# Moving the split weight tiles by multiples of 32 bytes in an fp32r decoder trunk on one core

## The chip, the core and the metric

The kernel runs on one NeuronCore of one Trainium2 chip, as one launch. The metric is the device time of one execution in microseconds (us). The whole of the core's work is done in one program: the sync engine (SP) issues nearly all loads, the tensor engine (PE) multiplies, the scalar engine (ACT), the vector engine (DVE) and GpSimd (POOL) prepare operands and take results out of PSUM.

## What is computed

The reference is a two-layer decoder trunk on 256 tokens of width 2048, in fp32. Layer 0 mixes by a gated spatial projection beside a 4-head attention into 256 memory tokens, layer 1 by 12-head latent attention beside the same kind of memory attention; after each comes an output projection and a gated feed-forward with a short causal convolution. Cut to the places where the weights enter:

```python
for l in range(DEPTH):                        # DEPTH = 2, N_A = 1
    if l == N_A:
        kv = rmsnorm(x, g_kv) @ w_kv_a
        ...
    h = rmsnorm(x, g_mix[l])
    ...
        z = h @ w_in_a[l]                     # 2048 x 3584 in layer 0, w_in_b 2048 x 1024 in layer 1
    ...
    mo = memory_attention(q_m, mem, g_mem[l], w_mem_kv[l])
    x = x + jnp.concatenate([main, mo], axis=-1) @ w_out[l]                    # 2048 x 2048
    x = x + conv_ffn(rmsnorm(x, g_ffn[l]), w_ffn_up[l], ..., w_ffn_down[l])    # 2048 x 11264, 5632 x 2048
return rmsnorm(x, g_final)
```

Nearly all arithmetic is in these projections: every weight is used once for 256 tokens.

## The kernel before, in words

**Split operands.** The data type fp32r runs through the PE in one pass but keeps fewer bits than fp32. The kernel therefore writes each fp32 operand as a sum of two fp32r numbers, high and low, and adds three products: high by high, high by low, low by high. Activations are split once per layer and stay in SBUF as one tile per use (`xhl`, `h`, `mainhl`, `memhl`, `qhl`, `chl`): per block of 128 features 512 columns, 256 tokens high and then 256 tokens low.

**Weights.** A weight is loaded, split and used in chunks of 128 partitions by at most 1024 columns (4096 bytes a partition). `chunk` (L92) does it: SP loads a `raw` tile (L101), ACT copies it into `whi` (L111, or L116 with a gain), which rounds it to fp32r, and DVE subtracts and writes the rest into `wlo` (L112, or L117). The three tags `raw`, `whi` and `wlo` have four buffers each in the pool `wp`, used in turn. Tiles of one tag lie one behind the other, and a tile may start at any multiple of 32 bytes of a partition. In the built program all twelve buffers begin 96 bytes past a multiple of 512, and so does every activation tile that the fp32r products read. The `whi` buffers are at 63072, 67168, 71264 and 75360, the `wlo` buffers at 79456 and on, each 4096 further.

**Products.** A projection is a slice of a weight matrix of 512 columns (or fewer), one call of `gemm_fm` (L171) or `gemm_tm` (L212); there are 99 such calls, of 96 or 128 matmuls each in the large ones. In `gemm_fm` the weights are the stationary operand (128 by 128) and the activations stream: `mm_fm` (L147) issues for each block a wide matmul of 512 columns, `whi` by high and low activations at once (L152), and a narrow one of 256 columns, `wlo` by the high activations into the second half of the same PSUM bank (L156). It issues all wide ones of two chunks, then all narrow ones, and turns the order for the next two chunks, so that 32 wide and 32 narrow matmuls alternate. In `gemm_tm` the activations are stationary and the weights stream, three matmuls of 512 columns for each block (L207, L208, L209); the memory values, the gate half of `w_in_a`, `w_uv` and the feed-forward's second matrix in layer 1 go this way. The queries of layer 1 call `chunk` directly, and one small block of `w_kv_a` goes through `stacked` (L123), which puts both parts into one tile.

**Order.** A scheduler sets the order on each engine from the program's data dependencies; it does not look at addresses. Dependencies are kept by semaphores: a `whi` buffer is written again when the last wide matmul that reads it is done, a `wlo` buffer after its last narrow one, and `raw` is loaded again when both halves of the split have read it.

**Scratch.** The program reserves 16384 bytes of each partition at address 0 as scratch of dynamic DMAs, ahead of all tiles.

The functions that the change touches, with the lines of the profile:

Of the kernel before, what the change touches and what calls it, by code (L numbers as in the profile page):

```python
# [9 lines left out]
F32R = mybir.dt.float32r  # L10
# [6 lines left out]
P = 128  # L17
# [52 lines left out]
class Kernel:  # L70
    def __init__(self, ctx, tc, t, out):
        self.tc, self.nc, self.t, self.out = tc, tc.nc, t, out
        self.ctx = ctx
        self.n = 0
        pool = lambda name, bufs=1, **k: ctx.enter_context(tc.tile_pool(name=name, bufs=bufs, **k))
        self.cp = pool("cp")
        self.wp = pool("wp")
        self.ap = pool("ap")
        self.ps = pool("ps", 8, space=bass.MemoryType.PSUM)
# [12 lines left out]
    def chunk(self, src, nk, ncol, gains=None, heads=None, raw=None):  # L92
        nc, n = self.nc, nk * ncol
        loaded = raw is not None
        if not loaded:
            raw = self.wp.tile([P, 1024], F32, tag="raw", name=self.uid("raw"), bufs=4)
        hi = self.wp.tile([P, 1024], F32R, tag="whi", name=self.uid("whi"), bufs=4)
        lo = self.wp.tile([P, 1024], F32R, tag="wlo", name=self.uid("wlo"), bufs=4)
        view = lambda x: x[:, :n].rearrange("p (k c) -> p k c", k=nk)
        if not loaded:  # L100
            nc.sync.dma_start(out=view(raw), in_=src)  # L101
        if heads is not None:

            s = view(raw).rearrange("p k (h c) -> p k h c", h=2)
            for c0, c1 in ((0, heads), (heads, ncol // 2)):
                o = lambda x: view(x)[:, :, 2 * c0 : 2 * c1].rearrange("p k (h c) -> p k h c", h=2)
                nc.scalar.activation(o(hi), s[:, :, :, c0:c1], AF.Copy)
                nc.vector.tensor_tensor(o(lo), s[:, :, :, c0:c1], o(hi).bitcast(F32), ALU.subtract)
            return view(hi), view(lo)
        if gains is None:  # L110
            nc.scalar.activation(hi[:, :n], raw[:, :n], AF.Copy)  # L111
            nc.vector.tensor_tensor(lo[:, :n], raw[:, :n], hi[:, :n].bitcast(F32), ALU.subtract)  # L112
        else:
            for k in range(nk):
                s = slice(k * ncol, (k + 1) * ncol)
                nc.scalar.activation(hi[:, s], raw[:, s], AF.Copy, scale=gains[k])  # L116
                nc.vector.scalar_tensor_tensor(  # L117
                    lo[:, s], raw[:, s], gains[k], hi[:, s].bitcast(F32), ALU.mult, ALU.subtract
                )
        return view(hi), view(lo)  # L120


    def stacked(self, src, nk, ncol, gains):  # L123
        nc, n = self.nc, nk * ncol
        raw, full = (self.wp.tile([P, 1024], F32, tag="raw", name=self.uid("raw"), bufs=4) for _ in range(2))
        nc.sync.dma_start(out=raw[:, :n].rearrange("p (k c) -> p k c", k=nk), in_=src)
        v3 = lambda x: x[:, :n].rearrange("p (k c) -> p k c", k=nk)
        g3 = gains.rearrange("p (k a) -> p k a", a=1).to_broadcast([P, nk, ncol])
        nc.vector.tensor_tensor(v3(full), v3(raw), g3, ALU.mult)
        blocks = []  # L130
        for i, tag in enumerate(("whi", "wlo")):
            w = self.wp.tile([P, 1024], F32R, tag=tag, name=self.uid(tag), bufs=4)
            half = slice(i * nk // 2, (i + 1) * nk // 2)
            w4 = w.rearrange("p (k o c) -> p k o c", o=2, c=ncol)
            nc.scalar.activation(w4[:, :, 0, :], v3(full)[:, half, :], AF.Copy)
            nc.vector.tensor_tensor(w4[:, :, 1, :], v3(full)[:, half, :], w4[:, :, 0, :].bitcast(F32), ALU.subtract)
            blocks += [w[:, j * P : (j + 1) * P] for j in range(nk // 2)]
        return blocks
# [29 lines left out]
            low(jobs)  # L168


    def gemm_fm(self, src, kbs, nblk, rhs, evict, nk=2, gain=None, hooks={}, raw=None):  # L171
        accs = [self.psum() for _ in range(nblk)]
        together = 1 if raw is not None else 2
        chunks = list(range(0, len(kbs), nk))
        groups = [chunks[i : i + together] for i in range(0, len(chunks), together)]

        def split(group):
            jobs = []
            for c in group:
                g = None if gain is None else [gain(kbs[c + i]) for i in range(nk)]  # L180
                hi, lo = self.chunk(src(kbs[c], nk), nk, nblk * P, g, raw=raw if c == 0 else None)
                for b in range(nblk):
                    cols = slice(b * P, (b + 1) * P)
                    for i in range(nk):
                        kk = c + i
                        jobs.append((accs[b], hi[:, i, cols], lo[:, i, cols], rhs(kbs[kk]), kk == 0, kk == len(kbs) - 1))
            return jobs

        ready = []
        for n, group in enumerate(groups):  # L190
            ahead = groups[n : n + 2] if raw is not None else [group]
            for g in ahead[len(ready) :]:
                ready.append(split(g))
                for f in hooks.get(-1, ()) if g is groups[0] else ():
                    f()
            self.mm_fm(ready.pop(0), n % 2 if raw is None else 0)
            for c in group:
                for f in hooks.get(c // nk, ()):
                    f()
        for b in range(nblk):  # L200
            evict(b, accs[b])
# [9 lines left out]

    def gemm_tm(self, src, nkb, ncol, lhs, evict, nk=2, gain=None, hooks={}, late=0):  # L212
        accs = [self.psum() for _ in range(2)]
        nch = nkb // nk
        order = lambda *engines: self.tc.manual_schedule(engines=set(engines)) if late else nullcontext()
        ET = mybir.EngineType

        def half(c, tb, hi, lo):
            for i in range(nk):
                k = c * nk + i  # L220
                self.mm_tm(accs[tb][:, :ncol], lhs(k), tb, hi[:, i, :], lo[:, i, :], k == 0, k == nkb - 1)

        kept = []
        with order(ET.PE):
            for c in range(nch):
                g = None if gain is None else [gain(c * nk + i) for i in range(nk)]
                hi, lo = self.chunk(src(c * nk, nk), nk, ncol, g)
                half(c, 0, hi, lo)
                if c < nch - late:
                    half(c, 1, hi, lo)  # L230
                else:
                    kept.append((c, hi, lo))
                for f in hooks.get(c, ()):
                    f()
            with order(ET.DVE, ET.Activation):
                if late:
                    evict(0, accs[0])
                for c, hi, lo in kept:
                    half(c, 1, hi, lo)
                if not late:  # L240
                    evict(0, accs[0])
                evict(1, accs[1])
# [113 lines left out]
    def gain(self, name, k, n=1):  # L356
        c = self.g[name] + k
        return self.gT[:, c : c + n]
# [741 lines left out]
```

## Time and profile before

| what | value |
|---|---|
| median of the 2 runs shown | 2103.38 us (2102.95 to 2103.81) |
| the profiled execution's own time | 2103.8 us |
| its span, first to last instruction | 2102.1 us |
| granted TensorE clock over the span | 0.999 |
| PE busy | 2090.7 us, 99% |
| DVE, ACT, POOL busy | 1460.8, 1140.1, 395.6 us |
| DMA: loaded from HBM | 387.88 MB |

The span leaves 1.7 us of the profiled execution outside the program's instructions. A matmul's record is longer than the time to the next one, since matmuls are pipelined: a run of n equal matmuls that the timeline gives as one piece lasts n-1 steps and one whole record. What a matmul costs the PE is the step. The span falls into stages: the start, the memory keys and values and layer 0's mixer up to some 355 us, the first feed-forward up to 1080 us, layer 1's mixer up to 1360 us, the second feed-forward to the end.

### The profile page before, as it was taken

Reading aid. Unit: us, or ns where it says so; the run is one execution under the profiler, and the core shown is the slowest. Engines: PE = TensorE matmul, PEld = TensorE weight load, DVE = VectorE, ACT = ScalarE, POOL = GpSimd, SP = SyncE. Lnnn points to the kernel's source line nnn. Section 1 sums busy time; section 2 is a strip of 40 time slices with the busy share of each in tenths; the row PEclk is TensorE's granted clock in tenths of the full one; section 3 lists DMA queues with packets and bytes.
Section 4 is the critical chain, followed back from the end, with each engine's and each line's share of the span. In section 5 each row is a group of like instructions: output and inputs, shape, how many; then the busy total and the mean of one; then the engine's idle time right before and its main releaser. Section 6 shows DMA issues by size and latency. Waiting matters only on the chain.

```text
span 2102.1 us, 30987 instructions
## 1 busy us (share of the span) xinstructions
PE 2090.7 (99%) x11608; PEld 1830.2 (87%) x11608; DVE 1460.8 (69%) x2147; ACT 1140.1 (54%) x1743; POOL 395.6 (19%) x387
## 2 busy tenths in 40 slices
PE   9999999999999999999999999999999999999998
PEld 8888888888888888888888888888888888888886
DVE  6755767777756777567788875777775677746775
ACT  6754654556535655445555664456553565535554
POOL 0100133312101211012244121421210122101220
PEclk9999999999999999999999999999999999999999
DMA  8565555555555565555555534555655556565554
GB/s 275 194 219 158 159 195 186 188 191 191 188 193 188 182 199 189 191 186 188 188 191 181 176 106 158 184 189 180 191 193 196 183 188 192 195 195 190 181 190 151
DMA packets 208092, 392.01 MB, mean 186 GB/s; under 512 B 14334, under 2 KB 23876, under 8 KB 207812
## 3 DMA queue, kind: packets, MB, share of 16 engines
q1 hardware_dynamic: 207364, 388.98, 56.9%
q8 instruction: 91, 1.49, 0.3%
q10 hardware_dynamic: 576, 1.05, 0.1%
q14 instruction: 61, 0.50, 0.1%
HBM read 387.88 MB, written 2.10 MB: 186 GB/s over the span
## 4 chain that ended last, share of the span: by engine, by line
PE 99%; DMA 0%; DVE 0%; ACT 0%; SPq 0%; issue 0%; DVEq 0%; ACTq 0%
PE ps L152 51%; PE ps L156 27%; PE ps L207 6%; PE ps L209 6%; PE ps L208 6%; PE ps L934 0%; PE ps L932 0%; PE ps L560 0%; PE ps L595 0%; PE ps L417 0%; DMA mtok<-in_mem 0%; PE ps L964 0%; PE ps L745 0%; PE ps L857 0%; PE ps L584 0%; PE ps L1036 0%
## 5 line engine op out<-in xcount | busy, mean ns | idle before, releaser
L112 DVE TENSOR_TENSOR wlo<-raw,whi 128x1024 fp32r<-128x1024 f32 x660 | 844.3, 1289 | 476.3 <-ACT whi L111 350.7
L111 ACT ACTIVATE whi<-raw 128x1024 fp32r<-128x1024 f32 x660 | 697.1, 1058 | 702.7 <-PE ps L152 509.9
L152 PE MATMUL ps<-xhl,whi 128*128 128x512 f32 x3264 | 765.3, 390 | 0.0
L152 PEld LDWEIGHTS ps<-xhl,whi 128*128 128x128 f32 x3264 | 605.8, 188 | 121.0
L647 POOL TENSOR_TENSOR a<-js,rbc 128x256 f32<-128x256 f32 x176 | 229.0, 1313 | 1103.2 <-DVE js L249 1007.6
L156 PEld LDWEIGHTS ps<-xhl,wlo 128*128 128x128 f32 x3264 | 406.6, 192 | 8.6
L156 PE MATMUL ps<-xhl,wlo 128*128 128x256 f32 x3264 | 411.0, 283 | 0.0
L152 PE MATMUL ps<-h,whi 128*128 128x512 f32 x704 | 164.8, 390 | 0.0
L650 ACT ACTIVATE c<-a,cT 128x256 f32<-128x256 f32 x176 | 105.1, 598 | 92.7 <-POOL a L647 91.3
L152 PEld LDWEIGHTS ps<-h,whi 128*128 128x128 f32 x704 | 130.6, 188 | 26.0
L208 PE MATMUL ps<-wlo,h 128*128 128x512 f32 x352 | 136.8, 389 | 0.0
L207 PE MATMUL ps<-whi,h 128*128 128x512 f32 x352 | 136.6, 389 | 0.0
L209 PE MATMUL ps<-whi,h 128*128 128x512 f32 x352 | 136.3, 389 | 0.0
L152 PE MATMUL ps<-mainhl,whi 128*128 128x512 f32 x512 | 120.2, 390 | 0.0
L152 PEld LDWEIGHTS ps<-mainhl,whi 128*128 128x128 f32 x512 | 94.9, 188 | 18.9
L652 DVE SCALAR_TENSOR_TENSOR c<-a,cT,c 128x254 f32<-128x254 f32 x176 | 101.1, 587 | 0.0
L117 DVE SCALAR_TENSOR_TENSOR wlo<-raw,gT,whi 128x512 fp32r<-128x512 f32 x112 | 87.1, 819 | 18.7 <-ACT whi L116 17.1
L651 DVE SCALAR_TENSOR_TENSOR c<-a,cT,c 128x255 f32<-128x255 f32 x176 | 91.5, 539 | 9.0 <-ACT c L650 8.9
L116 ACT ACTIVATE whi<-raw,gT 128x512 fp32r<-128x512 f32 x112 | 74.7, 721 | 32.0 <-PE ps L152 14.6
L249 DVE TENSOR_TENSOR js<-ps,cr 128x256 f32<-128x256 f32 x209 | 82.4, 416 | 12.2 <-POOL a L647 12.2
L156 PEld LDWEIGHTS ps<-h,wlo 128*128 128x128 f32 x704 | 87.7, 191 | 2.0
L156 PE MATMUL ps<-h,wlo 128*128 128x256 f32 x704 | 88.4, 283 | 0.0
(258 smaller groups left out, 1852.8 us busy)
## 6 DMA issues: line engine op xcount, KB each, us to landing
raw<-in_w_ffn_up SPq DMA_DIRECT2D x352, 512.0 KB, 3.5
raw<-in_w_ffn_down SPq DMA_DIRECT2D x176, 512.0 KB, 4.3
raw<-in_w_out SPq DMA_DIRECT2D x64, 512.0 KB, 3.4
raw<-in_w_in_a SPq DMA_DIRECT2D x56, 512.0 KB, 3.6
raw<-in_w_mem_kv SPq DMA_DIRECT2D x31, 512.0 KB, 4.7
raw<-in_w_in_b SPq DMA_DIRECT2D x16, 512.0 KB, 3.5
raw<-in_w_kv_a SPq DMA_DIRECT2D x9, 512.0 KB, 4.3
raw<-in_w_uq SPq DMA_DIRECT2D x12, 384.0 KB, 3.4
```

The costliest lines, as they stand in the source:

```text
L111: nc.scalar.activation(hi[:, :n], raw[:, :n], AF.Copy)
L112: nc.vector.tensor_tensor(lo[:, :n], raw[:, :n], hi[:, :n].bitcast(F32), ALU.subtract)
L117: nc.vector.scalar_tensor_tensor(lo[:, s], raw[:, s], gains[k], hi[:, s].bitcast(F32), ALU.mult, ALU.subtract)
L152: mm(acc[:, :], wh, x, start=first, stop=last)
L156: mm(acc[:, S:], wl, x[:, :S], start=False, stop=False)
L207: mm(acc, xh, wh, start=first, stop=False)
L208: mm(acc, xh, wl, start=False, stop=False)
L209: mm(acc, xl, wh, start=False, stop=last)
L647: nc.gpsimd.tensor_tensor(a, self.join(acc), rb, ALU.mult)
L650: nc.scalar.activation(c, a, AF.Identity, scale=w(2), bias=w(3))
L651: nc.vector.scalar_tensor_tensor(c[:, 1:], a[:, : S - 1], w(1), c[:, 1:], ALU.mult, ALU.add)
L652: nc.vector.scalar_tensor_tensor(c[:, 2:], a[:, : S - 2], w(0), c[:, 2:], ALU.mult, ALU.add)
```

## The change

`whi` and `wlo` tiles get 1088 columns in place of 1024, so a buffer has 4352 bytes a partition. `chunk` uses a slice of 1024 columns of it that starts at column `self.off`. A new function sets this offset at the start of each call of `gemm_fm` and `gemm_tm`: 0, 8, 16 ... 56 columns (0, 32 ... 224 bytes) in turn, so that every eighth projection has the same one. `stacked` always uses the first 1024 columns, and the queries of layer 1, which call `chunk` themselves, use the offset of the projection that was begun last. The scratch of dynamic DMAs is cut from 16384 to 4096 bytes, which makes room.

```diff
-        self.n = 0
+        self.n = self.projections = self.off = 0
...
-        hi = self.wp.tile([P, 1024], F32R, tag="whi", name=self.uid("whi"), bufs=4)
-        lo = self.wp.tile([P, 1024], F32R, tag="wlo", name=self.uid("wlo"), bufs=4)
+
+        hi, lo = (
+            self.wp.tile([P, 1088], F32R, tag=g, name=self.uid(g), bufs=4)[:, self.off : self.off + 1024] for g in ("whi", "wlo")
+        )
...
-            w = self.wp.tile([P, 1024], F32R, tag=tag, name=self.uid(tag), bufs=4)
+            w = self.wp.tile([P, 1088], F32R, tag=tag, name=self.uid(tag), bufs=4)[:, :1024]
...
+    def next_offset(self):
+        self.off = 8 * (self.projections % 8)
+        self.projections += 1
+
     def gemm_fm(self, src, kbs, nblk, rhs, evict, nk=2, gain=None, hooks={}, raw=None):
+        self.next_offset()
         accs = [self.psum() for _ in range(nblk)]
...
     def gemm_tm(self, src, nkb, ncol, lhs, evict, nk=2, gain=None, hooks={}, late=0):
         accs = [self.psum() for _ in range(2)]
+        self.next_offset()
...
-    nc = bacc.Bacc("TRN2", target_bir_lowering=False, num_devices=1)
+    nc = bacc.Bacc("TRN2", target_bir_lowering=False, num_devices=1, dynamic_dma_scratch_size=4096)
```

No instruction is added, removed or moved: on each of the five engines the two built programs hold the same instructions in the same order with the same waits. What differs is addresses. All tiles behind the scratch start 12288 bytes lower, those behind the weight buffers 10240 bytes lower, and in the built program `raw` and all activation tiles of the fp32r products are still 96 bytes past a multiple of 512. The `whi` and `wlo` buffers now lie 4352 bytes apart, each 96 bytes past a multiple of 256, and the weights in them begin 0 to 224 bytes behind that. The fp32r matmuls of the new program, sorted by where their weights begin (bytes past a multiple of 256):

| weights begin at | 0 | 32 | 64 | 96 | 128 | 160 | 192 | 224 |
|---|---|---|---|---|---|---|---|---|
| L152 of before (and as many of L156) | 560 | 560 | 592 | 644 | 596 | 660 | 596 | 520 |
| each of L207, L208, L209 of before | 72 | 72 | 56 | 56 | 88 | 56 | 64 | 72 |

The 16 matmuls of `stacked` are at 96.

## The prediction

> **What bounds the kernel now.** I read the page's busy times and slices first, then its chain, then the waits, and last the pace of the matmuls in the timeline.
>
> ```profile
> PE 2090.7 (99%) x11608; PEld 1830.2 (87%) x11608; DVE 1460.8 (69%) x2147; ACT 1140.1 (54%) x1743; POOL 395.6 (19%) x387
> ...
> PEclk9999999999999999999999999999999999999999
> ...
> PE 99%; DMA 0%; DVE 0%; ACT 0%; SPq 0%; issue 0%; DVEq 0%; ACTq 0%
> PE ps L152 51%; PE ps L156 27%; PE ps L207 6%; PE ps L209 6%; PE ps L208 6%; PE ps L934 0%; PE ps L932 0%; PE ps L560 0%; PE ps L595 0%; PE ps L417 0%; DMA mtok<-in_mem 0%; PE ps L964 0%; PE ps L745 0%; PE ps L857 0%; PE ps L584 0%; PE ps L1036 0%
> ```
>
> The PE works in every slice, at the full granted clock, and the chain that ended last is 99% PE: 96% of the span lies in the five fp32r lines L152, L156 and L207 to L209. The other engines wait for it, as the two longest waits of the splits show:
>
> ```profile
> ACT whi L111 <- PE ps L152: 509.9, 336, 6.9
> DVE wlo L112 <- ACT whi L111: 350.7, 210, 5.1
> ```
>
> ACT sat idle 509.9 us until wide matmuls gave a `whi` buffer back, and DVE waited mostly for ACT. So the time is the number of matmuls times their step. Two undisturbed pieces of PE's timeline give the steps, and the count by line stands behind them:
>
> ```profile
> 506.09 7.44 PE L152 MATMUL ps<-xhl,whi 128*128 128x512 f32 x32
> 513.38 4.00 PE L156 MATMUL ps<-xhl,wlo 128*128 128x256 f32 x32
> ```
> ```profile
> L152 PE MATMUL ps<-xhl,whi x3264: 387/389/586, 172.8 to 2027.3; 128*128 128x512 f32 x192
> L156 PE MATMUL ps<-xhl,wlo x3264: 277/283/468, 176.4 to 2023.8; 128*128 128x256 f32 x192
> ```
> ```profile
> 0.00:2102.10 2102.10, 1114.09 (x4728) 1.00 0.57 186
> 0.00:2102.10 2102.10, 598.37 (x4728) 1.00 0.57 186
> 0.00:2102.10 2102.10, 207.59 (x536) 1.00 0.57 186
> ```
>
> The last three rows are L152, L156 and L207 over the whole span (L208 and L209 have 536 each too); of them only the counts matter. A piece of 32 has 31 steps and one record of 389 or 283 ns (the medians above). A wide step is (7440 - 389)/31 = 227.5 ns, a narrow one (4000 - 283)/31 = 119.9 ns. The wide kind, with the 16 of the stacked block, is 4728 + 3 x 536 + 16 = 6352 matmuls: 6352 x 227.5 = 1445 us. The narrow kind is 4728 x 119.9 = 567 us. Together 2012 of 2102 us; the rest is fp32 matmuls, transposes, the start and the tail.
>
> The steps hide one thing more. 256 columns more cost 227.5 - 119.9 = 107.6 ns, so 512 columns are worth 215.2 ns and each matmul has 12.3 ns that don't depend on its width. Over 6352 + 4728 = 11080 matmuls that is 136 us. It is the only part of the step that a new place of the weights could plausibly take away, and what it is made of the trace does not say, since every fp32r operand of before lies 96 bytes past a multiple of 512.
>
> **The change part by part.** No instruction is added or moved, and no wait: the order and the waits are the same on all engines. There are four effects to price, all of them of addresses.
>
> *Addresses above 512 bytes move* (buffers 4352 apart, everything 10 or 12 KB lower). Cost nothing. The kernel before has eight starts of a weight block within 4 KB, four buffers, and operand tiles in five places, and the pace doesn't see them. From the chain in order of time, the first and the last of the 24 pieces of just 32 wide matmuls among its 25 longest pieces:
>
> ```profile
> 180.43 7.28 PE ps L152 x32
> ...
> 1990.73 7.28 PE ps L152 x32
> ```
>
> All 24 last 7.28 us, in two layers, with the buffers and the activation tile in different places.
>
> *Weights begin 0 to 224 bytes further.* By the table in the change, 644 of 4728 blocks stay at 96 (both the wide and the narrow matmul of each) and 56 of 536 in the other three lines, and the 16: 1288 + 168 + 16 = 1472. So 9608 matmuls read weights from a new place within 256 bytes. The trace has no fp32r matmul there. The nearest rows are fp32 products of 256 columns in the memory attention, whose stationary tile (`mv`) lies 96 bytes past a multiple of 256 in layer 0 (first row) and 224 in layer 1 (second), with the streaming tile at 96 both times; in the third row they are at 96 and at 224 the other way round. Behind them the record of one:
>
> ```profile
> 225.32 1.89 PE L595 MATMUL ps<-pT,mv 128*128 128x256 f32 x8
> ...
> 1218.85 1.03 PE L595 MATMUL ps<-pT,mv 128*128 128x256 f32 x4
> 1219.71 1.03 PE L560 MATMUL ps<-kT,qm 128*128 128x256 f32 x4
> ...
> L595 PE MATMUL ps<-pT,mv x32: 377/379/382, 225.3 to 1263.8; 128*128 128x256 f32 x32
> ```
>
> Steps: (1890 - 379)/7 = 215.9 ns at 96, (1030 - 379)/3 = 217.0 ns at 224 and for the third. One nanosecond, which is what the rounding of 1.03 us allows. I take 0. The row is near in kind (same array, same weight load of 128 columns) but streams at half the fp32r rate, so it bounds weakly: 1.1 ns either way over 9608 matmuls is 11 us. The far ends are, below, all 12.3 ns taken away from all 9608, 118 us, and above, what the rivals give.
>
> *ACT writes `whi` and DVE writes `wlo` 32-byte steps further.* The cover first. In the first feed-forward:
>
> ```profile
> 355.00:1080.00 725.00, 725.00 (x4176) 642.07 (x4176) 513.47 (x718) 385.41 (x541) 138.02 (x112) 1.00 0.58 190
> 360.00:1100.00 740.00, 18.14 (x44) 1.00 0.58 190
> 1400.00:2102.00 702.00, 19.49 (x44) 1.00 0.58 186
> 360.00:1100.00 740.00, 337.43 (x263) 1.00 0.58 190
> ```
>
> The first row has PE, PEld, DVE, ACT and POOL in that order: DVE is free for 725 - 513 = 212 us. The last row is L112 in about that stage, 263 splits at 1.28 us, so a split could take 212/263 = 0.8 us more, 63%, before DVE would set the pace; ACT has more room. The two rows between are a DVE product (L665) whose tiles lie at 96 in the first feed-forward and at 0 in the second: 412 against 443 ns, a single one of the 44 being long. Nothing like 63%. Cost nothing; without that cover, each 0.1 us on a split would cost 660 x 0.1 = 66 us.
>
> *The scratch shrinks to a quarter.* Whether the queues use it no row says, so the cover decides:
>
> ```profile
> q1 hardware_dynamic: 207364, 388.98, 56.9%
> ...
> raw<-in_w_ffn_up SPq DMA_DIRECT2D x352, 512.0 KB, 3.5
> ...
>   DMA raw<-in_w_in_b: 2.6, 1
> ```
>
> A chunk of the usual shape lasts 8 x 227.5 + 8 x 119.9 = 2.78 us on PE. With four `raw` buffers a load has about three chunks, 8.3 us, and lands in 3.5; among all waits of the instructions on `raw`, one is for a load, 2.6 us. A load would have to take 4.8 us longer before anyone saw it. I take 0. In the Trainium skill, "SBUF — State Buffer", section "SBUF size: 192, 224, or 256?", this scratch is the ring of software-generated descriptors; all loads here stand in queues that the profile calls hardware_dynamic, so by the page it is idle memory too, and no run here shows it.
>
> The sum: 0 + 0 + 0 + 0 on the profiled execution's 2103.8 us (2102.1 of span and 1.7 around it). The median of the runs shown is 0.4 us lower, 2103.4 us, and that is the forecast: no change.
>
> **The rivals.**
>
> *A. The 12.3 ns are the price of a bad start.* Every weight block of before begins 32 bytes off a multiple of 64 and of 128. If a block is read in such units, a good start saves the extra one, and the steps become 215.2 and 107.6 ns. For it: a cost that is the same at 512 and at 256 columns looks like a start or a boundary, and the fp32 steps above, 215.9 ns for 256 columns, are almost exactly twice 107.6, so fp32 matmuls hardly pay it. Against it: those have the same start and don't pay. Time: at 0, 64, 128 or 192 lie 2 x 2344 + 3 x 280 = 5528 matmuls; 5528 x 12.3 = 68 us less, 2035 us. If only multiples of 128 help, 2 x 1156 + 3 x 160 = 2792 matmuls and 34 us, 2069 us.
>
> The Trainium skill gives this rival its weight: "TensorE: Matmul & The Clock Gate", section "Back-to-back issue gap", has a warm matmul follow the last after its columns at 2.4 GHz and 2.5 ns, 215.8 and 109.2 ns at these widths. The trace disagrees by 11.7 and 10.7 ns at a clock of 1.00, so by that page something here costs time that need not be. If half of the matmuls lost it, the estimate would be 5528 x 11.2 = 62 us less, 2041 us; the page names no such cost of a start, and no run here shows one.
>
> *B. Where the weights lie against the streaming operand matters, and the old place is the good one.* Now both begin at the same place within 512 bytes. The trace has a stretch in which wide matmuls are slower with all else equal, the first after a narrow run; here the first five of a piece of 32, and then the last 27 of another one:
>
> ```profile
> 506.09 1.32 PE L152 MATMUL ps<-xhl,whi 128*128 128x512 f32 x5
> ...
> 1704.65 6.28 PE L152 MATMUL ps<-xhl,whi 128*128 128x512 f32 x27
> ```
>
> (1320 - 389)/4 = 232.8 ns at the start and (6280 - 389)/26 = 226.6 ns behind it: the settled step is 6.2 ns shorter than the first ones. So weight loads and streaming do disturb each other, and settle. If other places keep them unsettled, 5524 wide matmuls off 96 pay up to 6.2 ns: 34 us, 2138 us. If the 4084 narrow ones pay it too, 60 us, 2163 us. It decides over 2% from 42/9608 = 4.4 ns on each matmul. Against it: the fp32 rows, which have both places and no difference, and that no wide piece of 32 deviates.
>
> *C. The feed breaks*: loads through a quarter of the scratch take four times as long, 14 us, for four buffers 3.5 us a chunk in place of 2.78, a quarter slower. Against it: the waits above.
>
> **How the numbers follow.** No change 0.60. A with all multiples of 64 0.14, with multiples of 128 alone 0.06. B with the wide matmuls 0.05, with both kinds 0.12. C 0.03. Faster by over 2%, below 2061 us, is A's first case: 0.14. Slower by over 2%, above 2145 us, is B's second and C: 0.15. Within 2%, about what a measurement of this kernel can tell from no change, the other three: 0.71. The range must leave out no more than 0.2; one side alone could go, but neither sign has the better row, so I keep both outer priced cases, 2035 and 2163 us, and leave out C.
>
> **What would show it.** Right: in the changed profile a piece of 32 wide matmuls still lasts 7.4 us and one of 32 narrow ones 4.0 us in every projection, L111 and L112 keep 1.06 and 1.22 us, PE stays at 99%. A shows as two paces that change from projection to projection with a period of eight, 215 and 227 ns. B shows as steps of 230 ns and more in seven of eight projections, C as PE idle behind `raw`. Wrong would be any projection whose pace differs from that of its neighbours; then the 0 of the second part is the step that failed.

## The result, and the profile after

The changed kernel takes 2124.68 us (median of 2 runs, 2124.40 to 2124.97) against 2103.38: a ratio of 1.0099 [1.0082, 1.0116], 21.3 us or 1.0% slower. That is inside the range of the prediction, but the interval leaves out a ratio of 1: it is a real loss and not the forecast of no difference. The profiled execution's span grew by 20.6 us, from 2102.1 to 2122.7.

From the page of the changed kernel: the busy times with their instruction counts, the clock in 40 slices, the chain, two rows of loads and splits, and the two largest lines of matmuls. The changed source is longer, so L152 and L156 of before are now L154 and L158, the splits L111 and L112 are L113 and L114, and L207 to L209 are L214 to L216.

```profile
PE 2111.3 (99%) x11608; PEld 1822.0 (86%) x11608; DVE 1458.9 (69%) x2147; ACT 1140.7 (54%) x1743; POOL 397.7 (19%) x387
...
PEclk9999999999999999999999999999999999999999
...
PE 99%; DMA 0%; DVE 0%; ACT 0%; SPq 0%; issue 0%; DVEq 0%
...
L114 DVE TENSOR_TENSOR wlo<-raw,whi 128x1024 fp32r<-128x1024 f32 x660 | 841.1, 1284 | 493.8 <-ACT whi L113 359.8
L113 ACT ACTIVATE whi<-raw 128x1024 fp32r<-128x1024 f32 x660 | 698.6, 1059 | 721.9 <-PE ps L154 521.3
L154 PE MATMUL ps<-xhl,whi 128*128 128x512 f32 x3264 | 780.2, 395 | 0.0
...
L158 PE MATMUL ps<-xhl,wlo 128*128 128x256 f32 x3264 | 405.2, 281 | 0.0
...
raw<-in_w_ffn_up SPq DMA_DIRECT2D x352, 512.0 KB, 3.5
```

The picture is that of before with one thing changed. There are as many instructions on each engine, PE works 99% of the span at the full granted clock, and the chain is PE. ACT, DVE and POOL are busy for the same time, a split lasts as long (1284 and 1059 ns against 1289 and 1058), and a load lands after 3.5 us as it did. The idle time in front of the splits grew (ACT waited 521.3 us for L154 in place of 509.9 for L152), so they are even less in the way. What grew is the PE's time for the same matmuls, and it did so without a wait: the mean record of the wide line went from 390 to 395 ns, that of the narrow line fell from 283 to 281.

Where this sits shows in the timeline of PE. In before every whole piece of 32 lasts 7.44 us if wide and 4.00 if narrow. The next rows are consecutive pieces of the changed kernel, in order of start; the columns are the start, the duration, and the line with the count. Three projections follow each other here: their weights begin at 96 bytes (from 391.35 us), 128 (from 413.58) and 160 (from 436.08). The wide piece at such a border holds 16 matmuls of each.

```profile
394.97 4.00 PE L158 MATMUL ps<-xhl,wlo 128*128 128x256 f32 x32
398.81 7.44 PE L154 MATMUL ps<-xhl,whi 128*128 128x512 f32 x32
406.09 4.00 PE L158 MATMUL ps<-xhl,wlo 128*128 128x256 f32 x32
409.92 7.55 PE L154 MATMUL ps<-xhl,whi 128*128 128x512 f32 x32
417.31 3.95 PE L158 MATMUL ps<-xhl,wlo 128*128 128x256 f32 x32
421.10 7.62 PE L154 MATMUL ps<-xhl,whi 128*128 128x512 f32 x32
428.56 3.95 PE L158 MATMUL ps<-xhl,wlo 128*128 128x256 f32 x32
432.35 7.62 PE L154 MATMUL ps<-xhl,whi 128*128 128x512 f32 x32
439.81 3.93 PE L158 MATMUL ps<-xhl,wlo 128*128 128x256 f32 x32
443.58 7.63 PE L154 MATMUL ps<-xhl,whi 128*128 128x512 f32 x32
451.05 3.80 PE L158 MATMUL ps<-xhl,wlo 128*128 128x256 f32 x32
```

As long as the weights lie where they lay before, the pieces last 7.44 and 4.00 us. With the weights 32 bytes further a wide piece lasts 7.62 us and a narrow one 3.95. The last two narrow pieces lie at the same place and last 3.93 and 3.80. So there is a pace for each place, it goes up for one kind and down for the other, and it isn't quite fixed even at one place.

For the whole trace I subtracted the start of each matmul from the start of the next one, and sorted these steps by how many bytes past their old place the weights begin, which the addresses in the built program tell. Mean steps in ns:

| weights further by | 0 | 32 | 64 | 96 | 128 | 160 | 192 | 224 | before |
|---|---|---|---|---|---|---|---|---|---|
| wide (L154) | 230.4 | 234.7 | 234.1 | 234.5 | 232.5 | 233.8 | 229.3 | 233.6 | 228.6 |
| narrow (L158) | 120.1 | 119.0 | 116.6 | 117.8 | 118.8 | 120.2 | 117.8 | 117.0 | 120.0 |
| L214 to L216 | 227.3 | 234.0 | 229.0 | 234.7 | 234.8 | 234.5 | 234.4 | 233.2 | 227.7 |

The matmuls that stayed in place kept their pace: the 644 wide ones of the first column have 230.4 ns in before too, and the 228.6 of the last column is the mean of all projections.

The sums of these steps, before and after, give the account of the loss: the wide matmuls went from 1080.8 to 1101.1 us (+20.3), those of L214 to L216 from 365.9 to 374.4 (+8.5), the narrow ones from 567.4 to 559.7 (-7.7). Together +21.1 us, which is the 20.6 us of the span within 0.5.

### The profile page after: what moved, and what is told of

It reads as the page before. It is cut to its first block, busy times and chain, and to the rows that moved or that the text cites. A ratio compares the mean times of both kernels' runs of the same rounds, so it can differ in the third digit from the quotient of the medians.

```text
span 2122.7 us, 30987 instructions
## 1 busy us (share of the span) xinstructions
PE 2111.3 (99%) x11608; PEld 1822.0 (86%) x11608; DVE 1458.9 (69%) x2147; ACT 1140.7 (54%) x1743; POOL 397.7 (19%) x387
## 4 chain that ended last, share of the span: by engine, by line
PE 99%; DMA 0%; DVE 0%; ACT 0%; SPq 0%; issue 0%; DVEq 0%
PE ps L154 52%; PE ps L158 26%; PE ps L215 6%; PE ps L216 6%; PE ps L214 6%; PE ps L942 0%; PE ps L940 0%; PE ps L568 0%; PE ps L603 0%; PE ps L425 0%; PE ps L972 0%; PE ps L753 0%; DMA mtok<-in_mem 0%; PE ps L865 0%; PE ps L963 0%; PE ps L592 0%
## 5 line engine op out<-in xcount | busy, mean ns | idle before, releaser
L114 DVE TENSOR_TENSOR wlo<-raw,whi 128x1024 fp32r<-128x1024 f32 x660 | 841.1, 1284 | 493.8 <-ACT whi L113 359.8
L113 ACT ACTIVATE whi<-raw 128x1024 fp32r<-128x1024 f32 x660 | 698.6, 1059 | 721.9 <-PE ps L154 521.3
L154 PE MATMUL ps<-xhl,whi 128*128 128x512 f32 x3264 | 780.2, 395 | 0.0
L154 PEld LDWEIGHTS ps<-xhl,whi 128*128 128x128 f32 x3264 | 605.6, 188 | 134.9
L655 POOL TENSOR_TENSOR a<-js,rbc 128x256 f32<-128x256 f32 x176 | 231.0, 1324 | 1115.7 <-DVE js L257 1020.0
L158 PEld LDWEIGHTS ps<-xhl,wlo 128*128 128x128 f32 x3264 | 401.0, 189 | 9.5
L158 PE MATMUL ps<-xhl,wlo 128*128 128x256 f32 x3264 | 405.2, 281 | 0.0
L154 PE MATMUL ps<-h,whi 128*128 128x512 f32 x704 | 167.7, 394 | 0.0
L154 PEld LDWEIGHTS ps<-h,whi 128*128 128x128 f32 x704 | 130.5, 188 | 28.8
L214 PE MATMUL ps<-whi,h 128*128 128x512 f32 x352 | 138.1, 393 | 0.0
L216 PE MATMUL ps<-whi,h 128*128 128x512 f32 x352 | 138.0, 394 | 0.0
L154 PE MATMUL ps<-mainhl,whi 128*128 128x512 f32 x512 | 122.2, 394 | 0.0
L154 PEld LDWEIGHTS ps<-mainhl,whi 128*128 128x128 f32 x512 | 94.9, 188 | 20.7
L257 DVE TENSOR_TENSOR js<-ps,cr 128x256 f32<-128x256 f32 x209 | 82.4, 417 | 12.3 <-POOL a L655 12.3
L158 PEld LDWEIGHTS ps<-h,wlo 128*128 128x128 f32 x704 | 86.7, 189 | 2.2
L158 PE MATMUL ps<-h,wlo 128*128 128x256 f32 x704 | 87.3, 281 | 0.0
```

Source lines behind the costliest of these rows:

```text
L154: mm(acc[:, :], wh, x, start=first, stop=last)
L158: mm(acc[:, S:], wl, x[:, :S], start=False, stop=False)
L214: mm(acc, xh, wh, start=first, stop=False)
L216: mm(acc, xl, wh, start=False, stop=last)
L655: nc.gpsimd.tensor_tensor(a, self.join(acc), rb, ALU.mult)
```

## The experiments

The theory after the result: the step of an fp32r matmul depends on where its weights lie against the operand that streams past them, within 256 bytes. The rivals: it is the weights' own address that counts; or the greater distance of the buffers, the lower addresses or the smaller scratch. Each diff is against the kernel before or the changed one, as named; fences are rows of PE's timeline in the first feed-forward. A kernel with an interval was timed in rounds; the others have one run, with the kernel before at 2103.66 us beside it.

**The parts of the change alone.** In the changed kernel all weights stay at the old place, with the wide buffers, the lower addresses and the small scratch kept:

```diff
-        self.off = 8 * (self.projections % 8)
+        self.off = 0
```

> The changed kernel with every offset at 0: buffers 4352 bytes apart and the scratch of 4 KB stay. If the relative place of weights and streaming operand within 256 bytes makes the loss, all fp32r matmuls are back at relative place 0: 2103 us (2100 to 2106), a piece of 32 wide matmuls 7.44 us, of 32 narrow ones 4.00 us. If the pitch of the buffers, the lower addresses or the scratch make it: 2125 us.

Measured: 2103.75 us, a ratio to before of 1.0 [0.9991, 1.001]. The pieces:

```profile
413.35 4.00 PE L158 MATMUL ps<-xhl,wlo 128*128 128x256 f32 x32
417.19 7.44 PE L154 MATMUL ps<-xhl,whi 128*128 128x512 f32 x32
```

Both have their old duration. The whole loss comes with the offset; buffers, addresses and scratch cost nothing. With buffers 4352 bytes apart, every other one lies 256 bytes further against the activations than in before, and its matmuls keep their pace: at this place 256 bytes more make no difference.

**The absolute place.** In the kernel before, 64 bytes are put ahead of everything, so weights and activations move together:

```diff
         self.cp = pool("cp")
+        self.pad = self.cp.tile([P, 16], F32, name="pad")
```

> The kernel before with 64 bytes of padding ahead of all large tiles: raw, weights and activations all begin 160 bytes past a multiple of 256, their places against each other unchanged. If the relative place counts: 2103 us (2100 to 2106), pieces of 7.44 and 4.00 us. If the absolute place of the weights counts, all matmuls go like those at 160 in the changed kernel (wide 234 ns, narrow 116.5): 6352 x 6.4 - 4728 x 3.5 = 24 us more, 2127 us.

Measured: 2103.62 us, 1.0 [0.9991, 1.001].

```profile
413.08 4.00 PE L157 MATMUL ps<-xhl,wlo 128*128 128x256 f32 x32
416.92 7.44 PE L153 MATMUL ps<-xhl,whi 128*128 128x512 f32 x32
```

Weights that begin 64 bytes further, at 160 past a multiple of 256, keep the pace if the streaming operand goes with them. In the changed kernel weights at 160 did not. The weights' own address isn't what counts.

**The activations alone.** The same pad behind the weights and ahead of the activations, again in the kernel before:

```diff
         self.ap = pool("ap")
+        self.pad = self.ap.tile([P, 16], F32, name="pad")
```

> The kernel before with 64 bytes of padding between the weight buffers and the activations: the weights stay at 96, the activations go to 160, so the weights lie 64 bytes behind them, as they do in the changed kernel at 32. If the relative place counts, the narrow step is 117.8 in place of 120.0 ns, the wide one 0.8 ns longer, the 1608 matmuls that stream weights some 6.5 ns longer: 4728 x (0.8 - 2.2) + 1608 x 6.5 = 4 us more, 2107 us (2100 to 2114), a narrow piece of 32 lasts 3.93 us. If the absolute place of the weights counts, nothing changes: 2103 us, narrow piece 4.00 us.

Measured: 2102.25 us, 0.9993 [0.9984, 1.0002]. By the time alone nothing happened. The trace says otherwise:

```profile
402.72 3.93 PE L157 MATMUL ps<-xhl,wlo 128*128 128x256 f32 x32
406.49 7.49 PE L153 MATMUL ps<-xhl,whi 128*128 128x512 f32 x32
413.82 3.79 PE L157 MATMUL ps<-xhl,wlo 128*128 128x256 f32 x32
417.45 7.49 PE L153 MATMUL ps<-xhl,whi 128*128 128x512 f32 x32
424.77 3.93 PE L157 MATMUL ps<-xhl,wlo 128*128 128x256 f32 x32
```

No weight moved, and all three kinds have new paces: wide 229.9 ns, narrow 116.2, L208 to L210 234.0. With the activations 64 bytes further, the weights lie 192 bytes past them (256 - 64), and the column for 192 of the table above has 229.3, 117.8 and 234.4. A place that was reached from the other side gives nearly the same three numbers, so it is the relative place. The sums explain the unchanged time: narrow -17.9 us, wide +6.3, streamed weights +10.2, in all -1.4. My expectation of a visible loss missed by the narrow steps, which came out 1.6 ns shorter than in the changed kernel. The alternation of 3.93 and 3.79 us in one projection shows why a mean for a place can miss: two paces hold at the same place. In a piece of 3.93 us the steps are 116 to 121 ns from the first to the last, in one of 3.79 us 112 to 115, so which pace a run of matmuls falls into is settled where it begins. What settles it the runs don't show.

**The two kinds at places of their own.** In the changed kernel `whi` stays at the old place and `wlo` goes 64 bytes further in `gemm_fm`, where the weights are stationary; `gemm_tm` keeps both at the old place:

```diff
-            ...[:, self.off : self.off + 1024] for g in ("whi", "wlo")
+            ...[:, o : o + 1024]
+            for g, o in (("whi", 0), ("wlo", self.off))
...
-    def next_offset(self):
-        self.off = 8 * (self.projections % 8)
-        self.projections += 1
+    def next_offset(self, stream=False):
+        self.off = 0 if stream else 16
...
-        self.next_offset()
+        self.next_offset(True)
```

> The changed kernel with fixed offsets: the high parts at 0 everywhere, the low parts 64 bytes further in the projections whose weights are stationary, 0 in the others. If each kind has its own good place and keeps it beside the other, the narrow step falls from 120.0 to 116.8 ns and the wide one stays: 4728 x 3.2 = 15 us less, 2088 us (2083 to 2095). If the two kinds can't be placed apart (the pace of one carries over into the other): 2103 us or more.

Measured: 2093.88 us, 0.9953 [0.9936, 0.9969], faster than both kernels.

```profile
411.85 3.93 PE L159 MATMUL ps<-xhl,wlo 128*128 128x256 f32 x32
415.61 7.44 PE L155 MATMUL ps<-xhl,whi 128*128 128x512 f32 x32
```

The wide pieces keep 7.44 us beside narrow ones at another place, so here the kinds can be placed apart. The gain is smaller than expected, since the narrow steps settled at 118.1 ns and not at the 116.6 of the changed kernel. All whole narrow pieces last 3.93 us here; in the changed kernel, with `whi` at 64 too, half of them lasted 3.8: once more two paces at one place.

With `wlo` on the eight offsets of the change in turn and `whi` fixed (the offset above as `8 * (self.projections % 8)`):

> High parts at relative place 0 in all projections, low parts at 0, 32 ... 224 in turn in the projections whose weights are stationary. If each kind has its own good places: every wide piece of 32 stays at 7.44 us, the narrow pieces differ with a period of eight as in the changed kernel: 120 ns at 0 and 160, 116 to 118 at 64, 96, 192 and 224. Mean gain 1.4 ns on 4728 narrow matmuls, 7 us: 2097 us (2092 to 2101). If the narrow place carries over into the wide pace: wide pieces of 7.5 us and more in seven of eight projections, 2103 to 2120 us.

Measured: 2098.3 us. The wide steps are 228.8 ns on the mean, and whole wide pieces last 7.43 to 7.47 us beside every narrow place. The narrow ones by place, 0 to 224: 119.6, 118.9, 117.9, 118.1, 120.6, 120.2, 118.0, 116.6 ns. This is the gain of the change without its loss.

**How fine a place counts.** The changed kernel with steps of one column, 4 bytes:

```diff
-        self.off = 8 * (self.projections % 8)
+        self.off = self.projections % 8
```

> The changed kernel with offsets of 0, 4 ... 28 bytes in place of 0, 32 ... 224. If the unit in which weights and streaming operand meet is 32 bytes: the relative place within it hardly counts, steps between those at 0 and at 32 of the changed kernel (wide 227 to 235 ns, narrow 119 to 120), 2103 to 2120 us. If the unit is 4 to 16 bytes, the steps differ among the eight as much as they do among the multiples of 32, in a pattern of their own, or a place shows that is better than all of these (wide under 224 ns).

Measured: 2120.76 us. By offset, 0, 4 ... 28 bytes: wide 230.5, 234.2, 231.7, 233.3, 233.5, 233.3, 230.6, 228.9 ns; narrow 120.1, 118.7, 116.6, 117.0, 118.7, 120.0, 118.8, 116.9. Whole pieces at an offset of 0 (first row) and 4 (second and third):

```profile
398.97 7.44 PE L154 MATMUL ps<-xhl,whi 128*128 128x512 f32 x32
...
421.24 7.61 PE L154 MATMUL ps<-xhl,whi 128*128 128x512 f32 x32
428.69 3.94 PE L158 MATMUL ps<-xhl,wlo 128*128 128x256 f32 x32
```

One element of 4 bytes does as much as 32 bytes do. Nothing about 32 is special.

So I let one kind go through all 64 places of 256 bytes and held the other. First `wlo` (the version with places of their own, `self.off = self.projections % 64`):

> High parts at relative place 0, low parts at 0, 4, 8 ... 252 bytes in turn, one place per projection whose weights are stationary. Wide pieces stay at 7.44 us in every projection. If the place counts down to one element, narrow pieces of 32 differ between neighbours 4 bytes apart, from 3.79 us (113 ns a step) to 4.0 (120), and a place is found at which both pieces of a projection take 3.79; mean step 118 ns, 2095 us (2091 to 2101). If only the 32-byte place counts, eight neighbours at a time have the same pace.

Measured: 2097.83 us, wide steps 228.7 ns, narrow ones 118.7 on the mean. Most places have one projection each here. The best are 76 bytes (113.8 ns) and 88 (114.0), while 72 and 80 have 118.3 and 118.6. The pieces at 76 are the second and third of these, with 72 ahead of them:

```profile
556.20 3.95 PE L159 MATMUL ps<-h,wlo 128*128 128x256 f32 x32
...
567.27 3.80 PE L159 MATMUL ps<-h,wlo 128*128 128x256 f32 x32
...
578.19 3.81 PE L159 MATMUL ps<-h,wlo 128*128 128x256 f32 x32
```

The same for `whi`, with `wlo` held:

> The same with the parts exchanged: low parts at 0, high parts at 0, 4, 8 ... 252. If 0 is one of the best places of the wide matmuls: no wide piece of 32 under 7.40 us, most at 7.5 to 7.7 (230 to 236 ns), mean 232.5, 4 ns over before on 4600 matmuls, 2121 us (2112 to 2130). If 0 is only the best of the multiples of 32: pieces under 7.3 us at some places.

Measured: 2121.96 us. The wide steps have a mean of 232.8 ns, and no place is below 227.0; the few that reach 227.0 to 227.5 are 120, 132, 144, 156 and 252 bytes. Here is one such piece (second) beside a usual one:

```profile
948.53 7.52 PE L155 MATMUL ps<-xhl,whi 128*128 128x512 f32 x32
...
959.72 7.42 PE L155 MATMUL ps<-xhl,whi 128*128 128x512 f32 x32
```

7.42 us is 0.02 less than the 7.44 of before. The old place was among the best for the wide kind and, with 120.0 ns, among the worst for the narrow one. Most common offsets therefore trade one against the other, and there are 1.3 times as many wide matmuls as narrow ones (6352 to 4728).

One place breaks that rule. The first two rows are from the run with steps of 4 bytes, with both kinds at 28 bytes; the third is from this run, in the second feed-forward, with `whi` at 28 and `wlo` at 0:

```profile
730.71 3.90 PE L158 MATMUL ps<-xhl,wlo 128*128 128x256 f32 x32
734.45 7.42 PE L154 MATMUL ps<-xhl,whi 128*128 128x512 f32 x32
...
1785.94 7.68 PE L155 MATMUL ps<-xhl,whi 128*128 128x512 f32 x32
```

The same wide place lasts 7.42 us beside one narrow place and 7.68 beside another, in every whole piece at it (seven and two), so a kind's good place can hang on where the other kind lies, and these two sweeps are not the whole map. With both at 28 neither kind's whole pieces are longer than before. No kernel was run with everything there; the steps at 28 against those of the same matmuls before (wide +0.9 ns, narrow -3.0, streamed weights +1.3) give an estimate of 8 us less than before.

**Whether it is the weight load.** Two theories on the mechanism were tried. If the weight load's reading meets the streaming operand's, less reading should disturb less; if a matmul has a fixed start, its length should not count. In the kernel before, all narrow products and the wide ones of all but the first and last block of a sum take 64 of 128 weight columns, so that half of these columns' work is left out:

```diff
-                mm(acc[:, :], wh, x, start=first, stop=last)
+                n = P if first or last else P // 2
+                mm(acc[:n, :], wh[:, :n], x, start=first, stop=last)
...
-                mm(acc[:, S:], wl, x[:, :S], start=False, stop=False)
+                mm(acc[: P // 2, S:], wl[:, : P // 2], x[:, :S], start=False, stop=False)
```

> The kernel before, leaving work out: where weights are stationary, only 64 of each 128 weight columns are loaded and multiplied, in all narrow matmuls and in the wide ones except the first and the last block of a projection. The streaming is the same. If the 12.3 ns that don't depend on a matmul's width are the weight load disturbing the stream, they halve with the load: wide 221 ns, narrow 114 ns, (4137 + 4728) x 6.2 = 55 us less, 2049 us (2040 to 2065). If they are a fixed cost of starting an fp32r matmul or of switching weights: 227 and 120 ns, 2103 us.

Measured: 2086.42 us.

```profile
413.81 7.52 PE L153 MATMUL ps<-xhl,whi 128*64 128x512 f32 x32
421.17 3.80 PE L157 MATMUL ps<-xhl,wlo 128*64 128x256 f32 x32
```

The narrow steps fell to 114.1 ns, which is what a halved fixed part would give (113.8). The wide ones rose to 231.0 (221 if halved, 227 if fixed). Neither theory is right for both kinds.

The other way round: 128 weight columns, but all of them read from the first column of each block, so that the products are that column's:

```diff
-                        jobs.append((accs[b], hi[:, i, cols], lo[:, i, cols], ...
+                        one = lambda w: w[:, i, b * P : b * P + 1].to_broadcast([P, P])
+                        jobs.append((accs[b], one(hi), one(lo), ...
```

> The kernel before, leaving work out: where weights are stationary, all 128 columns of a block are loaded from the block's first column (a step of 0), so the weight load reads the same 4 bytes of each partition 128 times; the number of loads, columns and matmuls is as before. If the weight load and the stream disturb each other where their addresses meet, the pace must change: with one word in place of a walk through 512 bytes they meet less, wide under 222 ns and narrow under 116 (2060 us or less), or, if every access to that word is in the way, far over 240 ns. If addresses don't enter into it beyond the start, 227 and 120 ns, 2103 us.

Measured: 2093.18 us.

```profile
411.70 3.81 PE L156 MATMUL ps<-xhl,wlo 128*128 128x256 f32 x32
415.35 7.56 PE L152 MATMUL ps<-xhl,whi 128*128 128x512 f32 x32
```

Start, length and count of the weights are those of before; only the walk through the addresses is gone. The record of a wide matmul's weight load stays at 188 ns. The narrow steps fell to 114.5 ns, the wide ones rose to 231.9. So the addresses behind the first enter into the pace too, which speaks against a price of the start alone. But fewer addresses do not simply mean a shorter step. Which of the PE's parts makes the pattern stays open.

**A better version.** If places are fixed, the kinds can each have their best one: `whi` at the old place, `wlo` 76 bytes further in `gemm_fm`. The diff is that of the first kernel with separate places, with 19 columns for 16:

```diff
-        self.off = 0 if stream else 16
+        self.off = 0 if stream else 19
```

> High parts at 0, low parts 76 bytes further in all projections whose weights are stationary: the place at which both narrow pieces of a projection were short among the 64 (113.8 ns a step). If a place fixes the pace: 4728 x (120.0 - 113.8) = 29 us less than before, 2074 us (2070 to 2082), all narrow pieces of 32 at 3.80 us. If the pace also hangs on how a run is entered, and one projection was luck: part of the pieces at 3.93, 2080 to 2096 us.

Measured: 2076.61 us (4 runs, 2076.37 to 2076.79), a ratio to before of 0.9872 [0.9857, 0.9887].

```profile
412.71 7.44 PE L155 MATMUL ps<-xhl,whi 128*128 128x512 f32 x32
419.99 3.80 PE L159 MATMUL ps<-xhl,wlo 128*128 128x256 f32 x32
```

All 126 whole narrow pieces of the trace last 3.80 or 3.81 us, all 110 wide ones 7.44. Narrow steps are 114.4 ns, 5.6 less than before; 4728 of them make 26.5 us, and the median fell by 27.0. This is faster than the kernel before by 1.3% and than the changed one by 48.1 us.

Last, `whi` at 252 as well, the best-looking of its places (first number of the pair, in columns):

```diff
-        self.off = 0 if stream else 19
+        self.off = (0, 0) if stream else (63, 19)
```

> As the last, with the high parts at 252 bytes in those projections, where the wide matmuls were at 227.1 ns with no slow ones after a narrow run (228.6 at place 0). If both kinds keep their pace beside each other: 4728 x 1.5 = 7 us less again, 2067 us (2062 to 2076), wide pieces of 32 at 7.40 us. If the place that suits one kind depends on the other's: wide pieces of 7.5 us and more or narrow ones of 3.9, 2080 to 2125 us.

Measured: 2077.72 us, 0.9877 [0.986, 0.9893].

```profile
414.49 7.42 PE L155 MATMUL ps<-xhl,whi 128*128 128x512 f32 x32
421.76 3.82 PE L159 MATMUL ps<-xhl,wlo 128*128 128x256 f32 x32
```

A whole wide piece gains 0.02 us, but the mean wide step is 228.3 ns where 227.1 was expected. The 4728 steps are 8.1 us above 226.6 ns each (the settled step of before), and 6.1 us of that lie in the first and the last matmul of each run of wide ones, of which there are some 200. Against the version before it, the wide steps sum to only 1.3 us less: they save 3.3 us in the first five matmuls of the runs and lose 1.4 in the last one and 0.5 between. The narrow steps are 115.0 ns in place of 114.4 and cost 2.8 us more. I found no gain here from moving `whi`.

## Why the prediction was right and where it was wrong

The time came out 21.3 us above the forecast and within its range of 2035 to 2163 us. The forecast's reason, that nothing happens, was wrong. That the time stayed so near is luck: a loss of 28.8 us and a gain of 7.7 lie under it, and the range, which was set by rivals on both sides, would have held nearly any mixture of the two. Step by step:

*What bounds the kernel* held. PE at 99%, no wait on the way, and the time is the count of matmuls times their steps: the sum of the steps grew by 21.1 us and the span by 20.6.

*Addresses above 512 bytes, 0:* right. With them alone the ratio is 1.0 [0.9991, 1.001].

*Weights 0 to 224 bytes further, "I take 0":* this step failed. Over the 9608 moved matmuls the measured price is 21.1 us, 2.2 ns each, twice the bound of 1.1 ns that I drew from the fp32 rows. Those rows were not a bound. They compared weights at 0 and 128 bytes past the streaming operand and saw 1.0 ns; fp32r matmuls at the same two places have 228.6 (before) and 232.5 ns if wide, 120.0 and 118.8 if narrow. The same distance that does next to nothing to an fp32 matmul does up to 3.9 ns here. That they "stream at half the fp32r rate" was noted in the prediction; it should have led me to drop them as a measure, and not to keep them as a weak bound. And 2.2 ns is itself a balance: +5.2 ns on each of 5524 wide matmuls (28.8 us), -1.9 on each of 4084 narrow ones (7.7 us).

*Writes of `whi` and `wlo`, 0:* right. The splits last 1059 and 1284 ns.

*Scratch, 0:* right. Loads land in 3.5 us, and the kernel with the small scratch and no offset has the time of before. The cover was read too well, though: the prediction counted one wait for a load, 2.6 us, where the full list of before has seven, 8.3 us together; in the changed kernel there are six, 6.9 us.

*Rival A*, a bad start of the weights, was wrong as put. Multiples of 64 and 128 are no better: where the weights begin at a multiple of 64 (further by 32, 96, 160 and 224), wide steps are 234.7, 234.5, 233.8 and 233.6 ns, and with both operands moved by 64 nothing changes at all. But its core, that part of the 12.3 ns can go by a new place, holds for the narrow kind: at 76 bytes 5.6 of them went. The Trainium skill, "TensorE: Matmul & The Clock Gate", section "Back-to-back issue gap", has a warm gap of columns/2.4 + 2.5 ns, which it calls that of an isolated matmul; for these widths that is an estimate of 109.2 and 215.8 ns. The trace still disagrees: the best mean of any new place is 113.8 ns for 256 columns and 227.0 for 512.

*Rival B*, that the place against the streaming operand matters and the old one is good, is what happened for the wide kind: priced with up to 6.2 ns and 34 us, measured 5.2 ns and 28.8 us. The step of 230 ns and more, which the prediction named as its sign, stands in six of the seven new places, and the seventh has 229.3. For the narrow kind it had the wrong sign, since the old place was a bad one there; its case with both kinds, 60 us, was out by that. I gave the wide case alone 0.05. The evidence against B that weighed most, the fp32 rows, was the one that carried nothing, while the row for it, 232.8 ns at the start of a wide piece and 226.6 behind it, gave the right size and, for the wide kind, the right picture. In the wide piece at 421.10 us of the changed kernel the steps alternate between 235 and 231 or 232 ns from the third to the last, while those of a piece of before come down to 226 or 227 after five. That weight loads disturb the stream was read into that row; it shows only that the first steps are longer. The runs with everything and with the activations alone moved by 64 bytes show that the place of one operand against the other counts, and not by which part of the PE.

The Trainium skill, "TensorE: Matmul & The Clock Gate", section "Step-by-step: what each phase is for", says that the PE has two independent read ports, so that loading the next weights takes no read bandwidth from the running matmul. By that one wouldn't expect the place of one operand against the other to count. Here it does: moving the activations by 64 bytes, with no weight moved, took the narrow step from 120.0 to 116.2 ns and that of L208 to L210 from 227.7 to 234.0. The runs don't show that it is the ports.

*Rival C* was wrong: the waits for loads did not grow, and PE stayed at 99%.

## What to carry to other kernels

Where a kernel is bound by the steps of fp32r matmuls, the place of the stationary against the streaming operand within 256 bytes is a parameter that no wait shows; here it was worth a loss of 1.0% or a gain of 1.3%. Look at the duration of whole pieces by kind, not at the total, which can stay the same while three paces change. Each kind (width, and which operand is stationary) has good places of its own, so a common offset, and above all a rotation through offsets, mostly mixed good with bad here. One run in which the place changes from projection to projection measures many of them at once. The best is then fixed and measured again as a whole kernel, with both kinds where they will lie, since a good place of one kind can be lost beside another place of the other. A row from another kind of matmul, however alike it looked, was no bound here.

## What the hardware showed that was not expected

- The step of an fp32r matmul depends on the relative place down to one element of 4 bytes: narrow steps of 113.8 ns at 76 bytes and 118.3 at 72; a wide piece of 7.44 us at 0 and 7.61 at 4.
- Whole pieces of 32 lasted 3.79 to 4.05 us for 256 columns and 7.42 to 7.68 for 512, over all places tried with full weight blocks; the means for streamed weights went up to 237.8 ns (4 bytes further). All this at a granted clock of 1.00 and with PE busy 99% of the span.
- At one place there can be two paces (3.93 and 3.79 us for narrow pieces in turn, with all steps of a piece at one of them), so the way a run is entered counts. A wide place of 28 bytes lasted 7.42 us with the narrow kind at 28 and 7.68 with it at 0.
- Fewer weight columns or fewer weight addresses made the narrow step shorter (114.1 and 114.5 ns) and the wide one longer (231.0 and 231.9).
